# Sliding-window attention: projections and output products handed out one tile at a time, one to a block

## The chip, the cores and the metric

One core of one Trainium2 chip. The metric is the device time in microseconds (us) of one execution of the whole program, a two-layer decoder trunk on 1040 positions. Of several runs the median is compared.

## The reference, cut to what matters

The trunk runs a mixer, a gated MLP, sliding-window attention and a second gated MLP. The change is in the attention layer:

```
def swa_mixer(h, wq, wk, wv, q_norm_w, k_norm_w, sinks, wo):      # h: 1040 x 1024
    q = rms_norm((h @ wq).reshape(b, l, kv, grp, d), q_norm_w) * (d ** -0.5)   # 16 heads of 64
    k = rms_norm((h @ wk).reshape(b, l, kv, d), k_norm_w)                      # 4 key heads
    v = (h @ wv).reshape(b, l, kv, d)
    ...                                       # 16 meta tokens attend to themselves
    # 8 blocks of 128 queries; each sees the meta tokens, its own block and the one before
    s_meta = jnp.einsum('bnikgd,bjkd->bnkgij', qb, km)
    s_band = jnp.einsum('bnikgd,bnjkd->bnkgij', qb, kband)
    p = sink_softmax(jnp.concatenate([s_meta, s_band], -1), sink[None, None, :, :, None, None])
    orr = einsum(p_meta, vm) + einsum(p_band, vband)
    return jnp.concatenate([om, orr], 1) @ wo
```

## The kernel before, in words

The attention layer is the function `swa`. It does the 16 heads in two groups, G = 0 and G = 1, of eight heads each: four query tiles `qg[G][t]` of 128 rows (two heads) by 1040 columns (positions), one key tile, one value tile. A projection (`project`) is three matrix products, one for each third of the columns; each product is 24 matmuls on TensorE (eight weight tiles, and three terms because an operand is split in a high and a low part). So a projected tile is 72 matmuls. An output product (`outputs`) takes four query tiles of one group as input, so it has 12 matmuls for a third of the columns, 36 for a tile. `gemm`, line 147, issues all of these.

`attend(G, hook)` walks over the eight blocks of 128 queries. Scores of block n+1 are issued (`scores`, line 1067: eight score matmuls, then the softmax on VectorE, ScalarE and GpSimd) before block n is finished (`turn`: eight transposes `ptp`, line 1096, and the copies `all` and `own`; `out_block`: transpose `pmp`, products `po` at lines 1122 and 1125, and the copy of the result back into `qg`, line 1128). After block n it calls `hook(n)`, which puts other TensorE work between the blocks:

- While group 0 attends, `projections(1)` is a generator that makes the key, value and query tiles of group 1, with `head_norms` (square, the matmul `qkp` of line 971, logarithm, exponential). It is advanced at blocks 0, 1, 3, 5 and 6.
- While group 1 attends, the output products of group 0 (eight tiles, in four pairs that share one weight load) are made at blocks 0, 2, 3 and 5, a pair at a time. At block 5 the split copies `yb` of the finished query columns of group 1 are made (eight tiles), and at blocks 6 and 7 the output products of group 1 for the first two thirds of the columns.

After the last block come the last third of the columns, and then the second MLP (`ffn`). Its first work on VectorE prepares sums of squares (line 741) and combined inputs `X` (lines 752 to 800).

Two pools matter. `big` has 24 buffers of a full tile and holds the inputs `x`, the query tiles, the split tiles `ya` and `yb` (eight each) and the eight tiles `h` of the sum. Each `h` tile is brought back from memory by a DMA before its first product is added (`L1184` before, `L1186` after, then the addition `L1188` or `L1190`). The ring `mm` of accumulators has two buffers in this stage: a third product can't start until the first has been added.

The text's order isn't the order that runs. A list scheduler orders each engine's instructions ahead of time; earlier text has priority, and work that is ready fills gaps. Each engine then runs its list strictly in that order.

Of the kernel before, what the change touches and what calls it, by code (L numbers as in the profile page):

```python
# [27 lines left out]
QCH = [(14, 334)] + CH[1:]  # L28
# [54 lines left out]
def trunk(tc, hT0, w_in, w_ab, w_out, w_q, w_k, w_v, w_o, w_up, w_down, vec, cst, out):  # L83
    nc = tc.nc
    pe, ve, ac, gp, sp = nc.tensor, nc.vector, nc.scalar, nc.gpsimd, nc.sync
    ctx = ExitStack()
    with ctx:
# [32 lines left out]
        def newbig(name, dtype=F32, pool=None):  # L120
            return (pool or big).tile([P, T], dtype, tag="big", name=name)
# [7 lines left out]
        def load_w(src, nk, name, eng=gp):  # L129
            raw = wp.tile([P, nk, P], F32, tag="wraw", name=name + "r")  # L130
            sp.dma_start(raw, src)
            hi = wp.tile([P, nk, P], F32R, tag="whi", name=name + "h")
            lo = wp.tile([P, nk, P], F32R, tag="wlo", name=name + "l")
            ac.copy(hi, raw)  # L134
            eng.tensor_tensor(lo, raw, hi.bitcast(F32), ALU.subtract)  # L135
            return hi, lo

        def gemm(w, xs, c0, n, ks=None, ring=None):
            hi, lo = w
            ps = aux("mm", ring) if ring else mmp()  # L140
            ks = list(range(len(xs))) if ks is None else ks
            last = len(ks) * 3 - 1
            i = 0
            for j, k in enumerate(ks):
                xh, xl = xs[k]
                for a, b in ((hi, xh), (hi, xl), (lo, xh)):
                    pe.matmul(ps[:, :n], a[:, j, :], b[:, c0:c0 + n], start=(i == 0), stop=(i == last))  # L147
                    i += 1
            return ps
# [19 lines left out]
        def split(dst_h, dst_l, src):  # L169
            ac.copy(dst_h, src)  # L170
            ve.tensor_tensor(dst_l, src, dst_h.bitcast(F32), ALU.subtract)  # L171
# [773 lines left out]
        def swa(h, sqp):  # L945
# [5 lines left out]
            with tc.tile_pool(name="l1", bufs=1, reuse_waits="tile") as lp:  # L951
# [29 lines left out]
                def project(w, name, cs=CH):  # L981
                    d = newbig(name)
                    for c0, n in cs:
                        ps = gemm(w, xs, c0, n)
                        ve.tensor_tensor(d[:, c0:c0 + n], ps[:, :n], rstd[:, c0:c0 + n], ALU.mult)
                    return d
# [105 lines left out]
                def turn(pr):  # L1092

                    tp = aux("ptp", "a")
                    for t in range(4):
                        pe.transpose(tp[:, t * P:(t + 1) * P], pr[:, t, :], ident)  # L1096
                    x, y = (lp.tile([P, 512], F32, tag="hl", name=nm, bufs=8) for nm in ("all", "own"))
                    four = lambda a: a.rearrange("p (t i) -> p t i", t=4)
                    ac.copy(x, tp)
                    ve.tensor_tensor(four(y), four(tp), U.unsqueeze(1).broadcast_to([P, 4, P]), ALU.mult)  # L1100
                    return x, y

                def out_block(G, n, pmq, pts):


                    tok = slice(NM + n * P, NM + (n + 1) * P)
                    tp = aux("pmp", "a")
                    pe.transpose(tp[:, :P], pmq.rearrange("p t s m -> p (t s m)"), ident)
                    pmt = lp.tile([P, P], F32, tag="pmt", name="pmt", bufs=2)
                    ac.copy(pmt, tp[:, :P])  # L1110
                    v = vraw[G][:, n, :]
                    if n:
                        d = lp.tile([P, P], F32, tag="vd", name="vd", bufs=2)
                        gp.tensor_tensor(d, v, vraw[G][:, n - 1, :], ALU.subtract)
                        use = [(0, vraw[G][:, n - 1, :]), (1, d)]
                    else:
                        use = [(1, v)]
                    po = aux("po", "a")
                    for j, w in use:
                        for s in range(2):  # L1120
                            vs = slice(64 * s, 64 * s + 64)
                            pe.matmul(po[vs, :], w[:, vs], pts[s][j], start=(j == use[0][0]), stop=False,  # L1122
                                      skip_group_check=True)
                    for t in range(4):
                        pe.matmul(po[:, t * P:(t + 1) * P], vm[G][:, t, :], pmt, start=False, stop=True,  # L1125
                                  skip_group_check=True)
                    for t in range(4):
                        ve.tensor_copy(qg[G][t][:, tok], po[:, t * P:(t + 1) * P])

                def attend(G, hook):  # L1130
                    def first(n):
                        pmq = lp.tile([P, 4, 2, NM], F32, tag="pmq", name="pmq", bufs=2)
                        return pmq, scores(G, n, pmq)

                    nxt = first(0)
                    for n in range(8):
                        pmq, prs = nxt
                        if n < 7:
                            nxt = first(n + 1)
                        out_block(G, n, pmq, [turn(pr) for pr in prs])  # L1140
                        if n == 0:
                            meta_queries(G)
                        hook(n)

                def projections(G):

                    ring = None if G else "a"
                    kr = project(load_w(w_k[G], KT, "wk"), f"kr{G}")
                    if G:
                        vr = project(load_w(w_v[G], KT, "wv1"), f"vr{G}")  # L1150
                    last = lambda: keys(G, kr)
                    for t in range(4):
                        yield
                        qg[G][t] = project(load_w(w_q[G * 4 + t], KT, "wq"), f"q{G}{t}", QCH)
                        gp.memset(qg[G][t][:, 0:14], 0.0)
                        last()
                        if G and t == 0:
                            values(G, vr)
                        last = lambda t=t: head_norms(qg[G][t], qn, "a" if t == 3 else ring, QCH)
                    yield  # L1160
                    if not G:
                        vr = project(load_w(w_v[G], KT, "wv1"), f"vr{G}")
                    last()
                    if not G:
                        values(G, vr)

                def tiles():
                    return [(newbig(f"yh{t}", F32R), newbig(f"yl{t}", F32R)) for t in range(4)]

                def parts(G, ys, cs):  # L1170
                    for c0, n in cs:
                        sl = slice(c0, c0 + n)
                        for t in range(4):
                            split(ys[t][0][:, sl], ys[t][1][:, sl], qg[G][t][:, sl])

                def outputs(G, ys, cs, pairs=range(4), eng=gp):
                    for i in pairs:
                        w = load_w(w_o[i, G], 8, "wo", eng)
                        for j in range(2):
                            if G == 0:  # L1180
                                ho.append(newbig(f"h{2 * i + j}"))

                                gp.memset(ho[-1][:, 8:14], 0.0)
                                sp.dma_start(ho[-1][:, 14:], hd[i + 4 * j][:, 14:])  # L1184
                            t = ho[2 * i + j]
                            for c0, n in cs:  # L1186
                                ps = gemm([x[:, 4 * j:4 * j + 4] for x in w], ys, c0, n)
                                ve.tensor_tensor(t[:, c0:c0 + n], ps[:, :n], t[:, c0:c0 + n], ALU.add)  # L1188

                for _ in projections(0):  # L1190
                    pass
                rest = projections(1)
                attend(0, lambda n: next(rest, None) if n in (0, 1, 3, 5, 6) else None)
                for _ in rest:
                    pass
                ya = tiles()
                parts(0, ya, QCH)
                yb = []

                def hook(n):  # L1200

                    if n in (0, 2, 3, 5):
                        outputs(0, ya, QCH, ((0, 2, 3, 5).index(n),))
                    if n == 5:
                        yb.extend(tiles())
                        parts(1, yb, QCH[:2])
                    if n > 5:
                        outputs(1, yb, QCH[:2], (2 * n - 12, 2 * n - 11))

                attend(1, hook)  # L1210
                parts(1, yb, QCH[2:])
                outputs(1, yb, QCH[2:], eng=ve)
            return ho[0::2] + ho[1::2]

        with ExitStack() as st:
# [78 lines left out]
```

## Time and profile before

| | |
|---|---|
| median of 3 runs | 2385.93 us (2381.71 to 2390.98) |
| the profiled execution | 2385.68 us, of which the span of instructions is 2383.9 us |
| group 0 attends, first score to last `po` | 1373.9 to 1516.1 us |
| group 1 attends | 1516.1 to 1641.0 us |
| last output products | to 1668.6 us |
| busy, TensorE / VectorE / ScalarE / GpSimd | 98 / 68 / 41 / 17% of the span |

Times of stages are counted from the start of the span. A row of the profile names the engine (PE is TensorE, DVE VectorE, ACT ScalarE, POOL GpSimd, SP the queue that issues DMAs), the source line and the tiles. A row of stretches gives, for each engine, busy microseconds and the number of instructions, then the granted TensorE clock (1.00 is full), and the load of the DMA engines. A full-precision matmul appears as two instructions there, so a score matmul pair that the order shows as two counts four.

### The profile page before, as it was taken

To read this page: it belongs to the slowest core of one execution; us is meant where nothing else is said; L and a number is where in the kernel's file an instruction comes from. 1 tells how busy PE (TensorE), PEld (TensorE's weight loads), DVE (VectorE), ACT (ScalarE), POOL (GpSimd) and SP (SyncE) were. 2 spreads that over 40 slices of the span, in tenths; PEclk is the share of its full clock that TensorE was granted. 3 is DMA by queue.
4 is the path that set the end of the run, shared out by engine and by line. 5 is a ranking of instruction groups with operands and counts; after the bars stand their busy time and mean duration, and the time that the engine had idled before them with its cause. 6 is when DMAs were issued, how large, how long until landed. Compare 5 with 4: busy or idle time off the path is not lost.

```text
span 2383.9 us, 39785 instructions
## 1 busy us (share of the span) xinstructions
PE 2324.3 (98%) x16000; PEld 2182.5 (92%) x16000; DVE 1615.8 (68%) x2799; ACT 973.4 (41%) x1952; POOL 408.2 (17%) x357
## 2 busy tenths in 40 slices
PE   8999999999999999999999999999899999999999
PEld 7989999999999999999999986778799999987887
DVE  8886745566877777777436466768977777778332
ACT  6544313434444444433116456656544444443110
POOL 1123323431000000012225233231000000002221
PEclk9999999999999999999999999999899999999999
DMA  4233534241222222154223110203222222234222
GB/s 139 79 128 121 170 111 138 76 161 72 89 81 81 81 76 76 63 188 139 66 60 129 45 36 19 89 27 116 81 89 81 81 81 77 72 142 169 76 67 102
DMA packets 93481, 224.83 MB, mean 94 GB/s; under 512 B 18672, under 2 KB 30264, under 8 KB 93296
## 3 DMA queue, kind: packets, MB, share of 16 engines
q1 hardware_dynamic: 93296, 222.28, 27.1%
q8 instruction: 126, 2.06, 0.3%
q14 instruction: 59, 0.48, 0.1%
HBM read 166.08 MB, written 56.15 MB: 93 GB/s over the span
## 4 chain that ended last, share of the span: by engine, by line
PE 84%; DVE 10%; ACT 3%; DMA 1%; issue 1%; POOL 0%; SPq 0%; ACTq 0%; DVEq 0%; POOLq 0%
PE mm L147 40%; PE A L825 20%; PE C L825 15%; PE scp L1067 1%; DVE qt L251 1%; PE po L1122 1%; DVE X L752 1%; PE qkp L971 1%; PE po L1125 1%; ACT xh L182 0%; DVE Xd L499 0%; DVE yl L171 0%; DVE fq L497 0%; DMA rb<-rq 0%; PE ptp L1096 0%
## 5 line engine op out<-in xcount | busy, mean ns | idle before, releaser
L825 PE MATMUL A<-X,whi 128*128 128x260 f32 (+1 forms) x2816 | 513.3, 283 | 5.6 <-ACT whi L814 3.2
L147 PE MATMUL mm<-y,wdh 128*128 128x346 f32 (+2 forms) x1760 | 471.0, 350 | 1.6 <-DVE r L903 1.6
L825 PEld LDWEIGHTS A<-X,whi 128*128 128x128 f32 x2816 | 434.0, 189 | 7.2 <-ACT whi L814 3.6
L825 PE MATMUL C<-X,whi 128*128 128x260 f32 (+1 forms) x2112 | 393.7, 285 | 7.8 <-DVE v L894 5.9
L825 PE MATMUL A<-X,wlo 128*128 128x260 f32 (+1 forms) x1408 | 392.6, 283 | 1.3 <-DVE wlo L815 1.3
L147 PEld LDWEIGHTS mm<-y,wdh 128*128 128x128 f32 x1760 | 315.1, 188 | 32.7 <-DVE r L903 2.0
L135 POOL TENSOR_TENSOR wdl<-wdr,wdh 128x512 fp32r<-128x512 f32 (+1 forms) x80 | 118.8, 1485 | 1311.7 <-ACT wdh L134 1302.4
L825 PEld LDWEIGHTS C<-X,whi 128*128 128x128 f32 x2112 | 330.7, 190 | 8.9 <-DVE v L894 6.3
L147 PE MATMUL mm<-y,wdl 128*128 128x346 f32 (+2 forms) x880 | 307.5, 350 | 0.6 <-POOL wdl L135 0.6
L825 PE MATMUL C<-X,wlo 128*128 128x260 f32 (+1 forms) x1056 | 297.5, 284 | 0.0
L825 PEld LDWEIGHTS A<-X,wlo 128*128 128x128 f32 x1408 | 264.2, 189 | 1.5 <-DVE wlo L815 1.5
L939 DVE TENSOR_TENSOR h<-mm,h 128x346 f32<-128x346 f32 (+2 forms) x200 | 115.9, 584 | 201.8 <-PE mm L147 201.0
L825 PEld LDWEIGHTS C<-X,wlo 128*128 128x128 f32 x1056 | 200.4, 190 | 0.0
L147 PEld LDWEIGHTS mm<-y,wdl 128*128 128x128 f32 x880 | 165.5, 188 | 16.8 <-POOL wdl L135 1.3
L815 DVE TENSOR_TENSOR wlo<-sa,whi 128x1024 fp32r<-128x1024 f32 x44 | 53.9, 1226 | 161.8 <-ACT whi L814 161.8
L134 ACT CAST wdh<-wdr 128x512 fp32r<-128x512 f32 (+1 forms) x80 | 53.1, 663 | 255.6 <-PE mm L147 221.9
L814 ACT CAST whi<-sb 128x512 fp32r<-128x512 f32 x88 | 54.7, 621 | 132.7 <-PE C L825 131.0
L147 PE MATMUL mm<-xl,wqkvh 128*128 128x346 f32 (+1 forms) x288 | 95.8, 333 | 1.4 <-DVE xl L183 1.4
L147 PE MATMUL mm<-xh,wqkvh 128*128 128x346 f32 (+1 forms) x288 | 96.3, 337 | 0.7 <-DVE row L269 0.7
L814 ACT CAST whi<-sa 128x1024 fp32r<-128x1024 f32 x44 | 46.1, 1048 | 115.7 <-PE A L825 115.0
L147 PE MATMUL mm<-xh,wqkvl 128*128 128x346 f32 (+1 forms) x288 | 93.0, 325 | 0.0
L928 ACT CAST y<-yf 128x346 fp32r<-128x346 f32 (+2 forms) x110 | 54.7, 536 | 93.1 <-DVE yf L927 73.7
(391 smaller groups left out, 5054.1 us busy)
## 6 DMA issues: line engine op xcount, KB each, us to landing
wg<-in_w_up SPq DMA_DIRECT2D x44, 512.0 KB, 3.2
wv<-in_w_up SPq DMA_DIRECT2D x44, 512.0 KB, 3.3
wdr<-in_w_down SPq DMA_DIRECT2D x48, 256.0 KB, 2.6
fy<-sg SPq DMA_DIRECT2D x22, 520.0 KB, 2.7
yf<-fy SPq DMA_DIRECT2D x22, 520.0 KB, 4.1
fy<-sg SPq DMA_DIRECT2D x22, 516.0 KB, 2.7
yf<-fy SPq DMA_DIRECT2D x22, 516.0 KB, 4.7
wdr<-in_w_down SPq DMA_DIRECT2D x32, 320.0 KB, 3.5
```

The costliest lines, as they stand in the source:

```text
L134: ac.copy(hi, raw)
L135: eng.tensor_tensor(lo, raw, hi.bitcast(F32), ALU.subtract)
L147: pe.matmul(ps[:, :n], a[:, j, :], b[:, c0:c0 + n], start=(i == 0), stop=(i == last))
L251: ve.scalar_tensor_tensor(d, buf[:, pad + c0 - i:pad + c0 - i + n], taps[W - 1 - i], tmp[:, :n], ALU.mult, ALU.add)
L752: last_lo[:] = [ve.tensor_tensor(lo, src, hi.bitcast(F32), ALU.subtract).ins]
L814: ac.copy(hi, src)
L815: ve.tensor_tensor(lo, src, hi.bitcast(F32), ALU.subtract)
L825: pe.matmul(ps[:, b, :q], a[:, at + k, :], x[:, c], start=(start and n == 0), stop=(n == 11), skip_group_check=not start)
L928: ac.copy(yh[:, s], yf[:, s])
L939: ve.tensor_tensor(hn[m][:, s], ps[:, :n], hn[m][:, s], ALU.add)
L971: pe.matmul(p2[:, :n], ct[:, C_BD:C_BD + P], sq, start=True, stop=True)
L1067: pe.matmul(ps[:, :nk], qg[G][t][r, tok], kx[G][r, cols], start=True, stop=True)
```

## The change

`projections(1)` yields once more, between the key and the value tile of group 1, and is advanced at every block. `outputs` becomes a generator that yields after each output tile instead of running a pair at once; a hook takes one tile at blocks 0 to 4 and 6, two at block 5, none at block 7. At block 5 the tiles `yb` now come ahead of the last three of the eight output tiles of group 0, where they came behind all of them.

```
                     if G:
+                        yield
                         vr = project(load_w(w_v[G], KT, "wv1"), f"vr{G}")
...
                 def outputs(G, ys, cs, pairs=range(4), eng=gp):
+
                     for i in pairs:
                         w = load_w(w_o[i, G], 8, "wo", eng)
                         for j in range(2):
...
                                 ve.tensor_tensor(t[:, c0:c0 + n], ps[:, :n], t[:, c0:c0 + n], ALU.add)
+                            yield
...
-                attend(0, lambda n: next(rest, None) if n in (0, 1, 3, 5, 6) else None)
+                attend(0, lambda n: next(rest, None))
...
+                early = outputs(0, ya, QCH)
                 def hook(n):
-                    if n in (0, 2, 3, 5):
-                        outputs(0, ya, QCH, ((0, 2, 3, 5).index(n),))
                     if n == 5:
                         yb.extend(tiles())
                         parts(1, yb, QCH[:2])
+                    for _ in range((1, 1, 1, 1, 1, 2, 1, 0)[n]):
+                        next(early)
                     if n > 5:
-                        outputs(1, yb, QCH[:2], (2 * n - 12, 2 * n - 11))
+                        for _ in outputs(1, yb, QCH[:2], (2 * n - 12, 2 * n - 11)):
+                            pass
```

What the scheduler makes of it, at three places. In the rows below, a name with its number is one tile, and the count at the end is of equal instructions in a row.

First, TensorE in the last blocks of group 1. In the kernel before, the end of block 5 and what follows it (`scp` scores of a later block, `ptp` transposes of the softmax, `po` the block's product, `mm` an output product of group 1):

```order
L1122 MATMUL po<-own,vd 64x512 x2
L1125 MATMUL po<-pmt,vm_14934 128x128 x4
L1067 MATMUL scp<-kx_14912,q_15443 128x272 x2
L1096 MATMUL ptp<-ct,sc 128x128 x4
L147 MATMUL mm<-yh_16919,woh 128x346
L147 MATMUL mm<-yh_16919,woh 128x334
L147 MATMUL mm<-yl_16920,woh 128x334
L147 MATMUL mm<-yh_16919,wol 128x334
L147 MATMUL mm<-yh_16921,woh 128x334
```

And in the changed kernel, the end of block 5, block 6 and the start of block 7:

```order
L1125 MATMUL po<-pmt,vm_15028 128x128 x4
L1067 MATMUL scp<-kx_15006,q_14890 128x272 x2
L1067 MATMUL scp<-kx_15006,q_15133 128x272 x2
L1096 MATMUL ptp<-ct,sc 128x128 x8
L1108 MATMUL pmp<-ct,pmq 128x128
L1067 MATMUL scp<-kx_15006,q_15349 128x272 x2
L1067 MATMUL scp<-kx_15006,q_15565 128x272 x2
L1122 MATMUL po<-all,vraw_15009 64x512 x2
L1122 MATMUL po<-own,vd 64x512 x2
L1125 MATMUL po<-pmt,vm_15028 128x128 x4
L1096 MATMUL ptp<-ct,sc 128x128 x8
L1108 MATMUL pmp<-ct,pmq 128x128
```

Between the end of block 2 and the end of block 7 of group 1 stood 122 product matmuls; now there is none. They stand behind block 7, where 171 became 372. In group 0 the stretches that end with blocks 0 to 7 had 109, 107, 12, 60, 0, 72, 0 and 72 product matmuls, and have 105, 111, 0, 68, 4, 72, 72 and 24; the stretch that ends with block 0 of group 1 had 132 and has 36.

Second, the queue that issues DMAs, around the `h` tiles (`wor` is an output weight, `wg` and `wv` are weights of the second MLP, `hd` is the copy of the sum in memory). Before:

```order
L131 DMA wor_16539<-in_w_o 128x1024
L1184 DMA h0_16071<-hd0_13426 128x1026
L1184 DMA h1_16116<-hd4_13430 128x1026
L1184 DMA h2_16355<-hd1_13427 128x1026
L1184 DMA h3_16400<-hd5_13431 128x1026
L1184 DMA h4_16545<-hd2_13428 128x1026
L1184 DMA h5_16590<-hd6_13432 128x1026
L1184 DMA h6_16829<-hd3_13429 128x1026
L1184 DMA h7_16874<-hd7_13433 128x1026
L131 DMA wor_16823<-in_w_o 128x1024
```

After:

```order
L1186 DMA h3_16494<-hd5_13431 128x1026
L1186 DMA h4_16639<-hd2_13428 128x1026
L131 DMA wor_16847<-in_w_o 128x1024
L131 DMA wor_17037<-in_w_o 128x1024
L131 DMA wor_17099<-in_w_o 128x1024
L838 DMA wg_17852<-in_w_up 128x1024
L838 DMA wv_17854<-in_w_up 128x1024
L1186 DMA h5_16802<-hd6_13432 128x1026
L1186 DMA h6_16853<-hd3_13429 128x1026
L1186 DMA h7_16992<-hd7_13433 128x1026
```

Three of the eight `h` tiles moved behind weights of the next stage. Their buffers in `big` are those of query tiles of group 1, and the DMA of `h5` waits for the split of `q11` after the last block.

Third, VectorE behind the last block (`q` copies of the block's result, splits `yl`, additions to `h` tiles). Before:

```order
L1128 COPY q12_15443<-po_17185 128x128
L1128 COPY q13_15659<-po_17185 128x128
L870 MEMSET r_17754 128x2
L1188 TENSOR_TENSOR h4_16545<-mm_17218,h4_16545 128x346
L741 TENSOR_TENSOR r_17508<-r_17508,sq_17513 128x516
```

After:

```order
L1128 COPY q12_15349<-po_17185 128x128
L1128 COPY q13_15565<-po_17185 128x128
L171 TENSOR_TENSOR yl0_16779<-q10_14890,yh0_16778 128x346
L171 TENSOR_TENSOR yl1_16781<-q11_15133,yh1_16780 128x346
L171 TENSOR_TENSOR yl3_16785<-q13_15565,yh3_16784 128x334
L171 TENSOR_TENSOR yl3_16785<-q13_15565,yh3_16784 128x346
L171 TENSOR_TENSOR yl2_16783<-q12_15349,yh2_16782 128x346
L171 TENSOR_TENSOR yl3_16785<-q13_15565,yh3_16784 128x346
L1190 TENSOR_TENSOR h5_16802<-mm_16805,h5_16802 128x334
L1190 TENSOR_TENSOR h5_16802<-mm_16819,h5_16802 128x346
L1190 TENSOR_TENSOR h5_16802<-mm_16833,h5_16802 128x346
```

The products `mm_16805` and `mm_16819` stand on TensorE during block 2 and hold both accumulators of the ring from there; the next one, `mm_16833`, stands behind block 7 and waits for the first of these additions. In the kernel before, the addition next to the copies was to `h4`, whose DMA stands ahead of block 0's end in the list above.

More of the change, by code (lines that the diff above doesn't have):

```diff
@@ L1149, in projections @@
                     if G:
+                        yield
                         vr = project(load_w(w_v[G], KT, "wv1"), f"vr{G}")
@@ L1188, in outputs @@
                                 ve.tensor_tensor(t[:, c0:c0 + n], ps[:, :n], t[:, c0:c0 + n], ALU.add)
+                            yield
                 for _ in projections(0):
@@ L1192, in swa @@
                 rest = projections(1)
-                attend(0, lambda n: next(rest, None) if n in (0, 1, 3, 5, 6) else None)
+                attend(0, lambda n: next(rest, None))
                 for _ in rest:
@@ L1198, in swa @@
                 yb = []
+                early = outputs(0, ya, QCH)
                 def hook(n):
-                    if n in (0, 2, 3, 5):
-                        outputs(0, ya, QCH, ((0, 2, 3, 5).index(n),))
                     if n == 5:
@@ L1206, in hook @@
                         parts(1, yb, QCH[:2])
+                    for _ in range((1, 1, 1, 1, 1, 2, 1, 0)[n]):
+                        next(early)
                     if n > 5:
-                        outputs(1, yb, QCH[:2], (2 * n - 12, 2 * n - 11))
+                        for _ in outputs(1, yb, QCH[:2], (2 * n - 12, 2 * n - 11)):
+                            pass
                 attend(1, hook)
                 parts(1, yb, QCH[2:])
-                outputs(1, yb, QCH[2:], eng=ve)
+                for _ in outputs(1, yb, QCH[2:], eng=ve):
+                    pass
             return ho[0::2] + ho[1::2]
```

## The prediction

> **What bounds the kernel now.** I read the page first, for the engines and the chain that ended last:
>
> ```profile
> PE 2324.3 (98%) x16000; PEld 2182.5 (92%) x16000; DVE 1615.8 (68%) x2799; ACT 973.4 (41%) x1952; POOL 408.2 (17%) x357
> PE 84%; DVE 10%; ACT 3%; DMA 1%; issue 1%; POOL 0%; SPq 0%; ACTq 0%; DVEq 0%; POOLq 0%
> ```
>
> TensorE carries the program, and the change removes none of its work. It can gain or lose only what TensorE waits. So next came the stretches of the attention layer (first and second head group, then its blocks 3 to 7 alone, two blocks without products, the last products, the entry of the second MLP), and the same with line 147, the products, alone:
>
> ```profile
> 1373.90:1516.10 142.20, 137.26 (x834) 105.82 (x834) 94.14 (x300) 85.66 (x312) 45.58 (x62) 0.99 0.12 43
> 1488.40:1497.20 8.80, 7.67 (x36) 4.21 (x36) 8.00 (x24) 6.80 (x21) 2.24 (x4) 0.81 0.00 0
> 1587.00:1641.00 54.00, 49.70 (x305) 35.53 (x304) 39.77 (x125) 35.33 (x131) 19.64 (x22) 1.00 0.09 30
> 1598.00:1606.20 8.20, 6.98 (x43) 3.90 (x43) 6.16 (x26) 6.72 (x33) 3.54 (x6) 1.00 0.00 0
> 1606.20:1614.10 7.90, 7.22 (x42) 3.67 (x41) 6.00 (x25) 5.92 (x27) 2.77 (x5) 1.00 0.01 2
> 1641.00:1668.60 27.60, 27.56 (x175) 27.04 (x174) 26.29 (x47) 17.45 (x27) 0.00 (x0) 1.00 0.57 208
> ```
>
> ```profile
> 1373.90:1516.10 142.20, 75.26 (x432) 67.65 (x432) 0.99 0.12 43
> 1587.00:1641.00 54.00, 21.54 (x123) 18.96 (x123) 1.00 0.09 30
> 1626.30:1641.00 14.70, 11.87 (x70) 10.70 (x70) 1.00 0.23 74
> ```
>
> A block without products takes 8.2 and 7.9 us, and no engine is full in it. Busy times of TensorE overlap at the ends, so a product is priced by its pitch: 24 matmuls in 3.81 us in the chain in order of time, 0.159 us each.
>
> ```profile
> 1330.38 3.81 PE mm L147 x24
> ```
>
> Blocks 3 to 7 of the second group, 54.0 us, hold 122 product matmuls (the stretch's edge adds one), 19.4 us; 34.6 us remain for five blocks. The waits of TensorE in the whole layer are short, but one:
>
> ```profile
> PE C L761 <- DVE r L741: 7.9, 1, 7.9
> PE ptp L1096 <- POOL sc L1088: 4.0, 4, 1.5
> PE scp L1067 <- DVE sc L1074: 2.2, 3, 0.9
> ```
>
> The 7.9 us lie at the entry of the second MLP. The others are the softmax ending late. So little is left to gain among the blocks, and the question is what the new order uncovers.
>
> **The change part by part.** No instruction of arithmetic or DMA is added; all prices are of place.
>
> *Blocks 3 to 7 of group 1 lose their 122 product matmuls.* The 19.4 us of products themselves return behind block 7 at the same pitch: nothing. The blocks then run on the softmax alone: a block's transposes wait for its softmax, and the scores two blocks on wait for those transposes to free the score buffers. The timeline of TensorE, over blocks 4 to 6 before, gives that cycle:
>
> ```profile
> 1598.04 1.19 PE L1067 MATMUL scp<-kx,q 64*128 64x272 f32 x8 [0.70 <-DVE sc L1074]
> 1607.70 0.73 PE L1067 MATMUL scp<-kx,q 64*128 64x272 f32 x4
> 1608.97 0.66 PE L1096 MATMUL ptp<-ct,sc 128*128 128x128 f32 x4 [0.55 <-POOL sc L1088]
> ```
>
> The last score pair of block 5 is the second half of the first row (from about 1598.5), that of block 6 is the second row: 9.2 us. The two blocks by their ends took 8.2 and 7.9 us, being the tail of a covered stretch that let scores run ahead. In a run of five the cycle counts, so four blocks at 9.2. The fifth has no successor: at least its own TensorE work, 14.7 - 70 x 0.159 = 3.6 us, at most a cycle; I take 7.6, near the cycle, since its softmax is as long as any. 36.8 + 7.6 = 44.4 against 34.6: **+9.8**. Ends: four at 8.0 and 6.0, +3.4; five at 9.2, +11.4.
>
> *The wait behind block 7.* With both accumulators full since block 2, TensorE has nothing it may start until `h5` has landed. Rows of before at the same place (VectorE, then ScalarE), and the landings of these DMAs and of weights:
>
> ```profile
> 1641.27 0.89 DVE L1128 COPY q<-po 128x128 f32<-128x128 f32 x4 [1.99 <-PE po L1125]
> 1641.59 1.63 ACT L170 CAST yh<-q 128x346 fp32r<-128x346 f32 x4 [1.42 <-DVE q L1128]
> ```
>
> ```profile
> L171 DVE TENSOR_TENSOR yl<-q,yh 128x346 fp32r<-128x346 f32 x13 | 7.5, 592 | 0.0
> L1188 DVE TENSOR_TENSOR h<-mm,h 128x346 f32<-128x346 f32 x21 | 10.8, 513 | 8.8 <-PE mm L147 8.8
> wor<-in_w_o SPq DMA_DIRECT2D x10, 512.0 KB, 3.5
> DMA to landing us min/median/max: 6.9/8.0/9.2
> ```
>
> From the last `po` (1641.0): copies end at 1642.16, +1.2; two splits (`yl0`, `yl1`) at 0.59, +1.2; the DMA of 513 KB; one addition, +0.5. The eight `h` DMAs, issued together, landed in 6.9 to 9.2 us (last row); a weight of the same size alone in 3.5. Here three follow each other, with two weights just ahead in the queue: I take 4.6, nearer to the lone one. **+7.5**. Ends: 6.4 with 3.5, 12.1 with 9.2. Queued behind this wait are all remaining products, thus everything. GpSimd's splits of the weights are done by then and wait for nothing here. The same wait is the main thing the order hides: before, these loads lay under block 0's products.
>
> *The clock after that wait.* Before has one idle time of this length, and its clock:
>
> ```profile
> 1671.50:1674.90 3.40, 0.95 (x9) 0.75 (x7) 3.40 (x7) 2.30 (x4) 0.00 (x0) 1.00 0.48 194
> 1674.95:1685.19 10.24, 4.81 (x18) 4.44 (x19) 9.33 (x16) 8.24 (x15) 0.00 (x0) 0.50 0.00 0
> ```
>
> The clock is halved from 1674.95 to 1685.19; TensorE worked in 4.8 us of that at half speed and lost 2.4. I take the same after the new wait: **+2.4** (0 to 3.4: up to two thirds of such a stretch worked in at half speed).
>
> *Group 0.* Products came in 5 of 8 blocks, with two bare blocks (4 and 6) and a nearly bare one (2). Now 2 and 4 are bare and 7 has a third of one. Its half-clock stretch at block 6 (granted 0.81 in the row of 1488.40) should go: 3.4 us at half, 1.7. One bare block fewer, 8.8 against about 7.5: 1.3. **-3.0**. Ends: eight blocks take 142.2 - 432 x 0.159 = 73.5 us beside products; at 8.2 each they would take 65.6, so -8; a new stall of the same kind in one block gives +2.
>
> *The seam.* Block 0 of group 1 keeps 36 of 132 product matmuls; its transposes follow its last scores with little between. One wait of the largest size in the list, **+1.5** (0 to 4).
>
> *The entry of the second MLP.* VectorE was busy 26.29 of the last 27.60 us before it and ran late: products end at 1668.6, the last addition starts at 1671.23, and the last sum that TensorE waits for at 1679.63.
>
> ```profile
> 1671.23 0.51 DVE L1188 TENSOR_TENSOR h<-mm,h 128x346 f32<-128x346 f32 x1
> 1679.63 0.70 DVE L741 TENSOR_TENSOR r<-r,sq 128x516 f32<-128x516 f32 x1
> ```
>
> Now 372 matmuls (59 us) stand there in place of 171 over nearly the same VectorE work, so it should be in time: **-2.0** of those 2.6. The 9 us from the addition to the last sum stay: the same 13 instructions stand between them in both orders. Ends: 0 and -7.9.
>
> Sum: 9.8 + 7.5 + 2.4 - 3.0 + 1.5 - 2.0 = **+16.2**. Against the profiled execution's 2385.68 (its median is 2385.93, 0.01% off): **2402 us**. What a measurement of this kernel can tell from no change is about 0.5%, 12 us.
>
> **A rule weighed.** Half clock also came without a long idle time: in block 6 of group 0, after gaps of 1.50 and 1.03 us,
>
> ```profile
> 1488.42 0.66 PE L1096 MATMUL ptp<-ct,sc 128*128 128x128 f32 x4 [1.50 <-POOL sc L1088]
> 1490.11 0.66 PE L1096 MATMUL ptp<-ct,sc 128*128 128x128 f32 x4 [1.03 <-POOL sc L1088]
> 1487.20:1490.60 3.40, 1.15 (x8) 0.84 (x8) 1.83 (x9) 3.40 (x13) 2.76 (x4) 1.00 0.03 8
> 1490.60:1494.00 3.40, 3.33 (x11) 1.92 (x11) 3.15 (x8) 2.98 (x10) 0.00 (x0) 0.50 0.00 0
> ```
>
> so 3.4 us with 1.15 of work were enough. The Trainium skill, "TensorE: Matmul & The Clock Gate", section "HAM oscillation — how this bites in real kernels", gives as its rule that there be no idle gap over about 3.4 us. By that rule the bare blocks, whose gaps in the rows above are under 1 us, could never halve the clock, and the sum stands; by this trace they can, if a softmax comes late, which is the third rival. The trace goes against the rule as worded.
>
> **The rivals.** (1) *Mild*: bare blocks at 8.0 us, the DMA at 3.5, group 0 gaining 6: 3.4 + 6.4 + 2.4 - 6 + 0 - 2 = +4, 2390 us. For it: 8.2 and 7.9 are measured; against: the 9.2 us cycle.
>
> (2) *No slower*: the longer product tail lets VectorE prepare the whole entry of the MLP. Its place is 1668.6 to 1685; its price is what TensorE loses there against a full stretch of the MLP:
>
> ```profile
> 1675.00:1700.00 25.00, 17.64 (x108) 16.86 (x109) 24.09 (x39) 17.67 (x31) 0.00 (x0) 0.73 0.12 43
> 1700.00:1725.00 25.00, 24.08 (x196) 23.38 (x195) 23.65 (x33) 12.93 (x18) 0.00 (x0) 1.00 0.19 64
> 1725.00:1750.00 25.00, 25.00 (x212) 25.00 (x211) 17.63 (x23) 10.00 (x14) 0.00 (x0) 1.00 0.29 107
> ```
>
> 104 and 16 matmuls of 0.118 us too few, 14 us, and 2.6 from the start of the 7.9 us wait (1672.4) to 1675: 16.8. If all goes, 16.2 + 2 - 16.8 = +1.4, 2387 us. It decides from 6.3 us recovered on (16.2 + 2 - 6.3 = 11.9, the 0.5%). Against: the sums need the last addition, which needs the last product, and 13 VectorE instructions follow it as before.
>
> (3) *Heavier*: late softmaxes halve the clock twice in the bare run (2 x 1.7) and the DMA takes 9.2 (+4.6): 2410 us. Against: clock 1.00 in both bare rows above.
>
> (4) *Faster*: group 0 gains 8, the entry 7.9, and the rest is at its low ends, 3.4 + 6.4 + 0 - 8 + 0 - 7.9 = -6, not even out of the 0.5%; more than that would need what no row shows.
>
> **How the numbers follow.** Forecast 0.54 (2397 to 2408), mild 0.18, no slower 0.08, heavier 0.16, faster 0.04. The low end takes in the mild case, the high end the heavier one with a little over: 2389 to 2413. Slower by over 0.5% (from 2398): forecast and heavier, 0.70; within: mild and no slower, 0.26; faster: 0.04.
>
> **What would show it.** Blocks 3 to 7 of group 1 with a spacing of 8 to 9.5 us and no product among them; one wait of TensorE of 6 to 12 us behind block 7, in line 147, released by the addition to `h` (line 1190), with `h5`'s DMA issued about 2.5 us after the last `po`; half clock after it; group 0 a few us shorter; the wait on line 741 5 to 8 us. Wrong if products turn up among those blocks, if that wait is under 4 us, or if group 0 shortens by over 8.

## The result, and the profile after

| | before | after |
|---|---|---|
| median of 5 runs | 2388.03 us (2381.71 to 2390.98) | 2416.87 us (2413.50 to 2418.29) |
| the profiled execution | 2385.68 us, span 2383.9 | 2418.29 us, span 2416.5 |

The changed kernel takes 1.0122 times as long, with a 95% interval of 1.0106 to 1.0138. Slower was forecast, but 2402 us and at most 2413. So the question is where 15 us more than the sum came from (16.4 us between the profiled executions: 32.6 us longer, 16.2 forecast).

The page of the changed kernel, busy times of the engines. No engine has other work than before (as many instructions on each), but TensorE's busy time grew by 13.4 us, and that with the same matmuls:

```profile
PE 2337.7 (97%) x16000; PEld 2191.3 (91%) x16000; DVE 1609.2 (67%) x2799; ACT 971.8 (40%) x1952; POOL 411.1 (17%) x357
```

The stretches of the attention layer in the changed kernel, in the columns of the rows shown of before: group 0 with block 0 of group 1; blocks 1 and 2; blocks 3 to 7; the wait behind block 7; the remaining products.

```profile
1376.70:1539.80 163.10, 157.00 (x954) 120.94 (x954) 108.49 (x363) 101.78 (x380) 49.80 (x64) 0.99 0.11 40
1539.80:1579.30 39.50, 39.42 (x253) 31.61 (x253) 21.84 (x80) 16.50 (x67) 12.51 (x15) 1.00 0.09 28
1579.30:1631.70 52.40, 39.10 (x183) 20.39 (x180) 31.81 (x112) 29.48 (x123) 13.20 (x21) 0.80 0.00 1
1631.70:1639.60 7.90, 0.04 (x1) 0.00 (x0) 4.05 (x12) 1.62 (x4) 0.31 (x3) 0.63 0.90 296
1639.60:1702.90 63.30, 61.40 (x373) 60.58 (x374) 38.18 (x59) 23.16 (x32) 9.61 (x4) 0.97 0.33 116
```

The same for line 147 alone, the first two stretches before and then the same two after (busy time and count on TensorE):

```profile
1373.90:1547.40 173.50, 98.83 (x564) 88.30 (x564) 0.99 0.14 50
1547.40:1587.20 39.80, 26.91 (x151) 23.51 (x151) 1.00 0.08 27
```

```profile
1376.70:1539.80 163.10, 85.51 (x492) 77.19 (x492) 0.99 0.11 40
1539.80:1579.30 39.50, 25.52 (x144) 22.47 (x144) 1.00 0.09 28
```

With a product at its pitch of 0.159 us, as in the prediction, each stretch splits into products and the rest:

| stretch | rest before, us | rest after, us | difference | forecast |
|---|---|---|---|---|
| ahead of the attention layer (1373.9, now 1376.7) | | | +2.8 | 0 |
| group 0 and block 0 of group 1 | 173.5 - 564 x 0.159 = 83.8 | 163.1 - 492 x 0.159 = 84.9 | +1.1 | -3.0 + 1.5 |
| blocks 1 and 2 | 39.8 - 151 x 0.159 = 15.8 | 39.5 - 144 x 0.159 = 16.6 | +0.8 | 0 |
| blocks 3 to 7 | 34.6 | 52.4 | **+17.8** | +9.8 |
| wait behind block 7 | 0 | 7.9 | +7.9 | +7.5 |
| products behind it | 27.4 - 171 x 0.159 = 0.21 | 63.3 - 372 x 0.159 = 4.15 | +3.9 | +2.4 |
| from the last product on | 2383.9 - 1668.6 = 715.3 | 2416.5 - 1702.9 = 713.6 | -1.7 | -2.0 |

The sum is 32.6 us, the difference of the two profiled executions. The first row has the same code on both sides and differs from run to run (1374.2 to 1376.9 in the changed kernel and the kernels of the experiments). Blocks 3 to 7, a run of bare blocks (blocks without products), miss their forecast by 8.0 us. All other rows miss theirs the same way, by 8.4 us together, of which 2.8 are the first row.

In the waits of TensorE from 1370 us to 1760 us the forecast ones are there (`h` and, a little shorter, `r`), and the wait for the softmax (`sc`), 4.0 us before, is now 9.5 and 2.0 us, 11.5 together, and the largest:

```profile
PE mm L147 <- DVE h L1190: 9.8, 4, 7.9
PE ptp L1096 <- POOL sc L1088: 9.5, 6, 3.0
PE C L761 <- DVE r L741: 6.9, 1, 6.9
PE ptp L1096 <- DVE sc L1086: 2.0, 1, 2.0
```

The timeline shows the first transposes of blocks 3 to 7: the spacing is 9.7, 10.7, 11.6 and 12.3 us where 9.2 was forecast.

```profile
1579.27 0.60 PE L1096 MATMUL ptp<-ct,sc 128*128 128x128 f32 x4
1589.01 0.66 PE L1096 MATMUL ptp<-ct,sc 128*128 128x128 f32 x4 [1.58 <-POOL sc L1088]
1599.70 1.11 PE L1096 MATMUL ptp<-ct,sc 128*128 128x128 f32 x4 [3.05 <-POOL sc L1088]
1611.34 0.66 PE L1096 MATMUL ptp<-ct,sc 128*128 128x128 f32 x4 [1.70 <-POOL sc L1088]
1623.64 1.11 PE L1096 MATMUL ptp<-ct,sc 128*128 128x128 f32 x4 [2.01 <-DVE sc L1086]
```

Four transposes (one row of four instructions) take 0.66 us at one place and 1.11 at another. The granted clock says why. Stretches by the clock, the first ahead of a half-clock one, and then the four half-clock ones of this part:

```profile
1596.30:1599.70 3.40, 0.35 (x4) 0.00 (x0) 1.29 (x7) 3.40 (x19) 1.15 (x1) 0.99 0.00 0
...
1599.70:1606.50 6.80, 6.70 (x23) 3.36 (x25) 4.41 (x14) 2.82 (x10) 1.62 (x3) 0.50 0.00 0
1613.30:1620.10 6.80, 6.34 (x21) 2.88 (x21) 4.65 (x16) 2.28 (x8) 0.65 (x2) 0.50 0.00 0
1623.50:1630.40 6.90, 5.92 (x17) 2.38 (x17) 1.67 (x4) 1.34 (x3) 1.72 (x4) 0.51 0.00 0
1633.80:1644.00 10.20, 4.40 (x15) 4.40 (x16) 2.92 (x7) 0.82 (x1) 0.21 (x2) 0.50 0.59 200
```

Three of them lie in the bare run, 20.5 of its 52.4 us; before, the same blocks ran at 1.00 throughout.

### The profile page after: what moved, and what is told of

It reads as the page before. It is cut to its first block, busy times and chain, and to the rows that moved or that the text cites. A ratio compares the mean times of both kernels' runs of the same rounds, so it can differ in the third digit from the quotient of the medians.

```text
span 2416.5 us, 39799 instructions
## 1 busy us (share of the span) xinstructions
PE 2337.7 (97%) x16000; PEld 2191.3 (91%) x16000; DVE 1609.2 (67%) x2799; ACT 971.8 (40%) x1952; POOL 411.1 (17%) x357
## 5 line engine op out<-in xcount | busy, mean ns | idle before, releaser
L147 PEld LDWEIGHTS mm<-y,wdl 128*128 128x128 f32 x880 | 165.4, 188 | 15.8
L831 ACT COPY u<-A 128x520 f32<-128x520 f32 (+1 forms) x88 | 52.1, 592 | 96.0 <-PE A L825 95.9
```

The source lines that it names most:

```text
L831: ac.copy(two(t), ps[:, :, :q])
```

## The experiments

Two questions were put: which part of the change starves the blocks of their products, and why the starved blocks take 52.4 us rather than 44.4.

### Which part of the change

The theory (A) was that the second split tiles `yb`, asked for ahead of the last three tiles of group 0, take the buffers that `h5` to `h7` need, so that no product can run until block 7 is done; all of the loss is then in the outputs part. First the changed kernel with all its draws (the tiles that a hook takes with `next(early)`) ahead of `yb`; for that the draw of block 6 moves to block 4:

```
                 def hook(n):
+                    for _ in range((1, 1, 1, 1, 2, 2, 0, 0)[n]):
+                        next(early)
                     if n == 5:
                         yb.extend(tiles())
                         parts(1, yb, QCH[:2])
-                    for _ in range((1, 1, 1, 1, 1, 2, 1, 0)[n]):
-                        next(early)
```

> The changed kernel, but all eight output tiles of group 0 are drawn by block 5 and ahead of the split tiles yb (draws 1, 1, 1, 1, 2, 2). Everything else of the change stays: one tile at a time, one to a block, projections and outputs. Theory A (the loss comes from one thing, the yb tiles that take the buffers of the last three h tiles, so that products stop after block 2): the run of bare blocks, the wait behind block 7 and the half clock all go; 2385 to 2391 us against 2386 to 2388 before, no wait in line 147 over 2 us, the last block of group 1 ends at 1636 to 1645 us. Rival B (handing out one tile at a time costs by itself, since the products of a pair no longer follow each other): most of the 29 us stay, over 2405 us.

Measured: 2382.03 us (2376.90 to 2386.15, 12 runs), ratio to before 0.9976 (0.9968 to 0.9984). The loss is gone, and what is left of the change is 0.24% faster than before. Its blocks 3 to 7, all engines and then line 147 alone:

```profile
1581.10:1641.40 60.30, 58.33 (x368) 45.36 (x368) 42.35 (x131) 35.45 (x131) 20.93 (x23) 1.00 0.11 36
```

```profile
1581.10:1641.40 60.30, 32.85 (x186) 28.88 (x187) 1.00 0.11 36
```

They hold 184 products (the edge adds two), and 60.3 - 184 x 0.159 = 31.0 us remain, less than the 34.6 of before. The clock is full, and the waits of the transposes for the softmax sank to one:

```profile
PE ptp L1096 <- POOL sc L1088: 1.4, 1, 1.4
```

Then each half of the change alone. The outputs half, with the projections as before (the added `yield` ahead of `vr` taken out, and the projections advanced at blocks 0, 1, 3, 5 and 6):

> The output products half of the change alone; the projections are handed out as before. Theory A: the whole loss is here. The order shows bare blocks from block 2 on, one more than in the changed kernel, so 2414 to 2424 us. Rival C (the projections, with the seam between the groups left thin, carry a good part, 10 us or more): 2396 to 2408 us.

Measured: 2416.46 us (2416.07 to 2419.20), ratio 1.0124 (1.0111 to 1.0137): all of the loss. Blocks 3 to 7 take 55.7 us with no product, the wait behind them 7.0:

```profile
1578.40:1634.10 55.70, 41.11 (x185) 20.36 (x185) 32.14 (x119) 32.75 (x139) 15.49 (x23) 0.82 0.02 5
1634.10:1641.10 7.00, 0.00 (x0) 0.00 (x0) 4.01 (x12) 1.62 (x4) 0.31 (x3) 0.74 0.87 277
```

And the projections half, with the output products in pairs as before:

```
-                    for _ in range((1, 1, 1, 1, 1, 2, 1, 0)[n]):
-                        next(early)
+                    if n in (0, 2, 3, 5):
+                        outputs(0, ya, QCH, ((0, 2, 3, 5).index(n),))
                     if n == 5:
                         yb.extend(tiles())
```

> The projection half of the change alone: the second group's projections are handed out one to a block of the first group, the output products stay in lumps as before. Theory A (all of the loss is in the outputs part; the outputs part alone gave 2416.5, the whole change 2416.9): 2380 to 2387 us, the same as the version with all draws ahead of the second tiles (2382.0), whose count of products between the blocks is the same. Rival (the projections cost in the seam, where the profiled run of the changed kernel shows 4.6 us more): 2389 to 2395 us.

Measured: 2383.47 us (2382.06 to 2385.06), ratio 0.9977 (0.9966 to 0.9988). That is the gain of the first experiment, and the seam rival falls. So handing out the output products a tile at a time brings nothing measurable even when it starves no block; the projections bring 0.23%, and the order of two pieces of `hook` (with the draw of block 6 that must go ahead with it) costs 1.5%.

### Why the starved blocks are so slow

Two theories for the 8.0 us: the clock, which idle matmuls would hold up, or a softmax that takes longer by itself. The first try put four idle matmuls into the first transpose buffer of each of these blocks (their result is overwritten by the transposes):

```
-                def turn(pr):
+                def turn(pr, idle=0):
                     tp = aux("ptp", "a")
+                    for _ in range(idle):
+                        pe.matmul(tp, ones, ct[:, 0:512], start=True, stop=True)
...
-                        out_block(G, n, pmq, [turn(pr) for pr in prs])
+                        out_block(G, n, pmq, [turn(pr, 4 if G and n > 2 and not s else 0) for s, pr in enumerate(prs)])
```

> The changed kernel with four idle matmuls of constants (128x512, full precision, about 0.42 us each at full clock) put into the accumulator of the first transposes of each of blocks 3 to 7 of group 1, overwritten by them; they add work of 1.7 us a block where TensorE idles some 5 us of each. Theory D (what the forecast of the bare run missed is the half clock, which slows the blocks' own matmuls and thus lengthens the softmax chain): the clock stays at 1.00 in the bare run, the spacing of blocks falls from 10.7 to 12.3 us to 9 to 9.8, blocks 3 to 7 take 44 to 48 us in place of 52.4, the time is 2408 to 2413 us. Rival E (the chain of VectorE, ScalarE and GpSimd in the new order is that long by itself): spacing 10.5 us or more even at full clock, 2415 to 2420 us.

Measured: 2414.89 us (2413.84 to 2417.89), ratio 1.0117 (1.0104 to 1.0130). The stretch of blocks 3 to 7:

```profile
1576.65:1628.70 52.05, 48.88 (x223) 23.19 (x221) 31.98 (x112) 30.36 (x123) 13.32 (x21) 1.00 0.00 1
```

The clock was held, at 1.00 for the whole stretch, but no time came back, because TensorE was now full itself: an idle matmul took 0.86 us, so four were 3.4 us of each block. The test decides nothing. It does bound TensorE's own work in a block: 10.95 us from transposes to transposes, less 3.4, is 7.5 us.

```profile
1591.78 1.09 PE L1098 MATMUL ptp<-ct,sc 128*128 128x128 f32 x8
...
1602.73 1.09 PE L1098 MATMUL ptp<-ct,sc 128*128 128x128 f32 x8
```

The same with 16 more idle matmuls behind block 7, to hold the clock through the wait for `h5`:

```
+                        if G and n == 7:
+                            fill = aux("fill", "a")
+                            for _ in range(16):
+                                pe.matmul(fill, ones, ct[:, 0:512], start=True, stop=True)
                         hook(n)
```

> As the kernel with idle matmuls in blocks 3 to 7, and 16 more of them (6.8 us at full clock) behind block 7, where TensorE waits 7.9 us for the h5 tile. Theory D: the wait itself stays as long (until the addition to h5), but the products behind it start at full clock: 2 to 2.5 us less than without the 16. If the clock after a wait is not held by work of this kind: no difference within 1 us, or some us more.

Measured: 2422.89 us (2421.79 to 2424.32), ratio 1.0149 (1.0135 to 1.0164), a miss: the 16 took 13.9 us, longer than the wait that they were to fill. The products behind them ran at full clock almost at once (0.32 us where they had taken 0.49).

```profile
1630.49 13.90 PE L1148 MATMUL fill<-ct 128*128 128x512 f32 x32
```

So next came two idle matmuls a block, that fit into the waits (`turn(pr, 2 if ...)`), and then the same with eight behind block 7 (`range(8)`):

> The changed order with two idle matmuls of 512 columns (0.86 us each in the run with four) into the first transpose buffer of blocks 3 to 7 of the second group: 1.7 us a block, which fits into the waits of 1.6 to 3.05 us that stand there. In the run with four, TensorE's own work at full clock with 3.4 us of idle matmuls filled a block of 10.95 us, so its own work is at most 7.5 us and work with two idle ones at most 9.3 us. Theory A (half clock makes the excess of the bare run over 9.2 us a block): no stretch of half clock from the start of block 3 to the last output product, a spacing of the blocks of 9.0 to 9.8 us, the bare run 44 to 48 us in place of 52.4, and 2408 to 2412 us. Theory B (the softmax itself takes 10.5 to 12 us a block when nothing lies beside it, and the half clock falls into waits): spacing 10.5 to 12 us with the waits for the softmax still there behind the idle matmuls, bare run 51 to 54 us, 2414 to 2418 us. Theory C (two idle matmuls don't hold the clock): half-clock stretches remain, 2414 to 2420 us.

> The one before, with eight more idle matmuls (6.9 us) behind block 7, where TensorE waits some 7.4 us for h5. If half clock behind that wait is worth the 2.2 to 2.4 us that the products lost there (forecast term +2.4), this is 1.5 to 2.5 us under the kernel with two idle matmuls alone, the stretch of half clock from about 1633 gone and the first products behind the wait at 0.32 us a pair, not 0.65. If the eight end later than h5's addition, or delay it, no difference or 1 us more.

Measured: 2412.90 us (2411.07 to 2414.51), ratio 1.0096 (1.0081 to 1.0111), and 2412.32 us (2410.83 to 2415.76), ratio 1.0092 (1.0075 to 1.0109). With two idle matmuls the blocks 3 to 7 took 48.5 us, and the first transposes of blocks 4, 5 and 6 follow each other at 9.1 and 9.0 us, full clock up to block 7 (the two values are just outside the ranges of theory A):

```profile
1579.90:1628.40 48.50, 41.68 (x203) 21.20 (x201) 31.46 (x112) 29.90 (x123) 13.32 (x21) 0.93 0.01 4
```

```profile
1591.00 0.66 PE L1098 MATMUL ptp<-ct,sc 128*128 128x128 f32 x4
1600.06 0.66 PE L1098 MATMUL ptp<-ct,sc 128*128 128x128 f32 x4
1609.08 0.66 PE L1098 MATMUL ptp<-ct,sc 128*128 128x128 f32 x4
```

That looked like the clock theory. But the compiled order had changed as well, and with it where the scores stand. So the next run shrank the two idle matmuls to 16 columns, next to no work; and one had a single idle matmul of full width, whose order has the scores late from block 5 on.

```
-                        pe.matmul(tp, ones, ct[:, 0:512], start=True, stop=True)
+                        pe.matmul(tp[:, 0:16], ones, ct[:, 0:16], start=True, stop=True)
```

> The kernel with two idle matmuls a block, but each of 16 columns in place of 512, so that they fill next to none of the waits. In the compiled order the idle matmuls also moved the scores: in the changed kernel both pairs of transposes of blocks 4 and 6 stand together with the last scores behind them, and its spacing behind block 4 was 10.7 us at full clock; with idle matmuls of either size the scores stand between the two pairs in block 4. So the run with two idle matmuls (2412.9 us, blocks 3 to 7 in 48.4 us) changed two things at once. Theory A (its 4 us came from the clock): half-clock stretches return, blocks 3 to 7 take 51 to 53.5 us, 2415 to 2418 us. Theory B (they came from the order of the scores among the transposes): spacings of 9.0 to 9.6 us up to block 5, blocks 3 to 7 in 45 to 49 us, 2408 to 2413 us.

> One idle matmul of 512 columns a block (0.86 us). In its compiled order block 4 has the scores between the transposes, block 5 has both pairs of transposes together and the last scores behind them. Theory B (order): from block 4 to 5 a spacing of 9.0 to 9.5 us, from 5 to 6 one of 10.3 to 11.5 us, at full clock in both; blocks 3 to 7 in 49 to 52 us, 2412 to 2416 us. Theory A (clock): the spacing does not follow the order, and every spacing over 10 us has a stretch of half clock in it.

Measured with the tiny ones: 2407.91 us (2404.18 to 2412.98), ratio 1.0084 (1.0071 to 1.0097). Blocks 3 to 7 take 44.3 us, and the wait behind them 6.8:

```profile
1578.00:1622.30 44.30, 33.74 (x200) 19.24 (x199) 30.20 (x112) 29.29 (x123) 13.16 (x21) 0.96 0.01 2
1622.30:1629.10 6.80, 0.00 (x0) 0.00 (x0) 4.04 (x12) 1.62 (x4) 0.31 (x3) 0.63 0.90 309
```

Against the changed kernel that is 8.1 us in the blocks and 1.1 in the wait, and the medians differ by 9.0. Idle work that keeps TensorE busy isn't needed; the order does it. The spacings by the first transposes are 9.8, 8.8, 7.9 and 10.0 us (9.0 to 9.6 up to block 5 expected by theory B, and 45 to 49 us for the five blocks); one stretch of half clock, 3.4 us, is left in block 7. The timeline of TensorE in block 4, the changed kernel first, then the one with the tiny idle matmuls (each with the first transposes of block 5 last; the rows between are left out). Eight score matmuls make a block, sixteen instructions here; counted back from the last ones, the row at 1591.39 holds the last four of block 5, and the row at 1589.17 the last two of block 5 and the first two of block 6.

```profile
1589.01 0.66 PE L1096 MATMUL ptp<-ct,sc 128*128 128x128 f32 x4 [1.58 <-POOL sc L1088]
1590.70 0.66 PE L1096 MATMUL ptp<-ct,sc 128*128 128x128 f32 x4 [1.03 <-POOL sc L1088]
...
1591.39 1.19 PE L1067 MATMUL scp<-kx,q 64*128 64x272 f32 x8
...
1599.70 1.11 PE L1096 MATMUL ptp<-ct,sc 128*128 128x128 f32 x4 [3.05 <-POOL sc L1088]
```

```profile
1587.96 0.66 PE L1098 MATMUL ptp<-ct,sc 128*128 128x128 f32 x4 [1.08 <-POOL sc L1088]
1589.17 1.19 PE L1067 MATMUL scp<-kx,q 64*128 64x272 f32 x8 [0.55 <-DVE sc L1074]
1590.29 0.65 PE L1098 MATMUL ptp<-ct,sc 128*128 128x128 f32 x4
...
1596.78 0.65 PE L1098 MATMUL ptp<-ct,sc 128*128 128x128 f32 x4
```

In the changed kernel the last scores of block 5 stand behind both pairs of transposes of block 4. The second pair waits for the second half of block 4's softmax, so these scores end at 1592.6, 3.6 us behind the first transposes, and the softmax that needs them takes until 1599.70, 7.1 us: a cycle of 10.7 us at full clock. With the scores between the two pairs the last of block 5 are done at about 1589.8, 1.8 us behind the first transposes; the next transposes start 7.0 us later, at 1596.78: a cycle of 8.8 us. The softmax is as long in both, and in this block the place of the scores makes the difference. VectorE confirms the count: its first maximum of block 5 starts about 1 us behind those scores, in the changed kernel and then with the tiny idle matmuls:

```profile
1593.79 0.75 DVE L1079 TENSOR_REDUCE sc<-sc 128x4 f32<-128x576 f32 x1
1590.59 0.75 DVE L1079 TENSOR_REDUCE sc<-sc 128x4 f32<-128x576 f32 x1
```

In blocks 5 and 6 of the changed kernel the last scores stand late as well.

The single idle matmul gave 2413.31 us (2407.55 to 2414.66), ratio 1.0101 (1.0086 to 1.0117), and blocks 3 to 7 in 48.2 us. Its spacings by the first transposes are 9.6, 8.9, 9.6 and 11.5 us. From block 4 to 5, the scores between the pairs, 8.9 was about as expected (9.0 to 9.5); from 5 to 6, the scores behind, 9.6 is longer but misses the expected 10.3 or more; and the 11.5 from 6 to 7, again with the scores behind, has a stretch of half clock in it. The five blocks are shorter than the 49 to 52 us expected. So the order sets the direction, and its price in one block is 0.7 to 1.9 us, not always the larger.

How the 8.1 us divide between longer waits and slower clock can be read roughly: of 52.4 us TensorE was busy 39.1 and idle 13.3; with the tiny matmuls 33.7 and 10.6. The waits are 2.7 us of it, and 5.4 (more, as the tiny ones themselves take some 0.4 us a block) is the same work at half clock: the late scores lengthen the gaps to as much as 3.05 us, and by this reading the gaps take the clock. What each would cost without the other wasn't tried, since every inserted instruction moved the order too. Nor was a `big` pool with more buffers, which would leave `h5` its own.

## Why the prediction was wrong, point by point

*The bare run of blocks 3 to 7, +9.8: the step that failed.* That the 122 products leave these blocks and that the softmax then sets the pace was right. The failed step is "In a run of five the cycle counts, so four blocks at 9.2": the 9.2 us were read from blocks 5 and 6 of before and taken over as a property of the softmax, though the cycle depends on where the last scores stand. In the changed order, printed above for block 6, the last scores of a block stand behind all eight transposes, and with them so 3.6 + 7.1 = 10.7 us was measured. Something near it could have been worked out beforehand. In before, block 6's last scores (1607.70 in the prediction's rows) end at 1608.4, and its first transposes start 7.3 us later:

```profile
1606.95 0.66 PE L1096 MATMUL ptp<-ct,sc 128*128 128x128 f32 x4
...
1615.73 0.66 PE L1096 MATMUL ptp<-ct,sc 128*128 128x128 f32 x4 [0.88 <-POOL sc L1088]
```

The second pair of transposes starts there 2.0 us behind the first (1608.97); with its 0.66 and 1.19 for four score matmuls behind it, the estimate is 3.9 + 7.3 = 11.2 us a block. With the last scores of each block ahead of the second pair (the tiny idle matmuls) the five blocks took 44.3 us, and the prediction had 44.4; that they agree so closely is in part luck, as the spacings run from 7.9 to 10.0 us and a stretch of half clock is among them. The second half of the failure is that the third rival's mechanism, half clock in the bare run, came with it: not two stretches worth 1.7 us each, but three that fill 20.5 us. The argument against it ("clock 1.00 in both bare rows") rested on gaps under 1 us, and the late scores made them longer. Measured +17.8.

*The wait behind block 7, +7.5: right.* 7.86 us, ended by the addition to `h5`. Its parts, in the order forecast, were off in opposite directions: the DMA of `h5` was issued at 1633.59, 1.8 us behind the last `po` (2.4 forecast), and the addition behind it started 5.45 us later (4.6), of which VectorE waited 3.77 us; that the total fits to 0.4 us is in part luck. TensorE, and then VectorE, there:

```profile
1639.60 0.66 PE L147 MATMUL mm<-yh,woh 128*128 128x346 f32 x1 [7.86 <-DVE h L1190]
```

```profile
1631.78 0.89 DVE L1128 COPY q<-po 128x128 f32<-128x128 f32 x4 [4.15 <-PE po L1125]
1632.62 2.65 DVE L171 TENSOR_TENSOR yl<-q,yh 128x346 fp32r<-128x346 f32 x6
1639.04 0.93 DVE L1190 TENSOR_TENSOR h<-mm,h 128x334 f32<-128x334 f32 x2 [3.77 <-DMA h<-hd]
```

*Half clock behind it, +2.4: right.* The clock was half from 1633.8 to 1644.0, the 15 products in that stretch took 4.4 us where they need 2.4: 2.0. The eight idle matmuls that filled this wait removed the half-clock stretch, and from the last `po` to the last product it took 68.8 us with them and 71.3 without: 2.5 us. The medians, 0.6 us apart, can't tell that much, and the profiled execution with the eight was 1.3 us longer than the one without, through a second MLP that is the same in both. The other 1.9 us of the +3.9 are three short waits for `h` (9.8 less 7.9 in the list), which were not in the sum.

*Group 0 and the seam, -3.0 and +1.5: too good by 2.6.* Together +1.1. The half-clock stretch of block 6 went, as forecast, but one came into block 7, from 1524.6 to 1528.0. The two terms should have been one: with the projections spread out, work moved across the boundary between them. The last matmul `qkp` of the head norms (line 971) started at 1523.6 before, in block 0 of group 1, and starts at 1514.8 now, within group 0. What each term measured by itself isn't known.

*The entry of the second MLP, -2.0: near in size, its reason not shown.* Measured -1.7. The time from the last product to the end differs by more than that among kernels with the same code there: 713.0 us with two idle matmuls a block, 716.4 with the eight behind block 7 as well. But the version with its draws ahead of `yb` and the one with the projections alone have 168 products at the end, three fewer than before, and gain as much in the entry: in the 125 us behind the last product TensorE does 905 matmuls before and 919 after, 918 with the draws ahead of `yb`, 919 with the projections alone and 919 with the tiny idle matmuls. More time for VectorE under a longer tail isn't what does it.

*The rule weighed.* The sum took the bare blocks to keep the clock, and left late softmaxes that halve it to the third rival. The trace went the rival's way: gaps of at most 3.05 us, with 0.35 of 3.40 us busy ahead of the first, halved the clock three times. The rule of the Trainium skill, "TensorE: Matmul & The Clock Gate", section "HAM oscillation — how this bites in real kernels", that no idle gap be over about 3.4 us, doesn't protect a kernel like this one: none of these gaps is that long.

## What to carry to other kernels

A cycle that is read from one place holds for the order of instructions at that place; when a change makes a loop run bare, write down the new order of its waiting instructions and add up the chain from it. A handful of small waits can cost more in clock than in waiting (here 5.4 against 2.7 us, read roughly), so when a stretch loses its cover, price its matmuls at half clock as well. And two requests for buffers of one pool are an order of priority: the one that comes first can starve work that was ready, here at a cost of 1.5%.

## What the runs showed that was not expected

- The half clock comes in stretches of 3.4, 6.8 or 10.2 us, and how many isn't fixed by the code: in block 7 of group 0, with the same order of instructions, it took 3.4 us in the changed kernel and about 6.8 and 10 us in the runs with tiny and with two idle matmuls, and the block took 19.5, 19.3 and 20.7 us. The Trainium skill, "TensorE: Matmul & The Clock Gate", section "Part 1: The HAM clock gate", has the activity counted in windows of about 3.4 us that run freely; the lengths agree with that, and the same gaps would then fall into these windows differently in each run.
- Two inserted matmuls of 16 columns a block moved the scores among the transposes, and the kernel became 9 us faster. A probe that adds an instruction must have its order compared before its time is read.
- A full-precision matmul of 128 x 512 took 0.86 us at full clock, in two records that follow each other at 0.43; the first expectations had it at one. A product matmul of 128 x 346 has a pitch of 0.159 us.
